# Bursts of transposes on one Trainium2 core: two chunks at once in the feed-forward stages, and a few heads later in the attention

## The chip, the core and the metric

The kernel runs on one core of a Trainium2 chip. Such a core has a matrix engine (TensorE, "PE" in the profile), three engines for elementwise work (VectorE "DVE", ScalarE "ACT", GpSimd "POOL"), and SyncE ("SP"), which here issues the DMA transfers. TensorE reads from the on-chip memory SBUF and writes to PSUM, a small memory of banks. Each engine works through its own list of instructions in order; an instruction that needs another engine's result waits for a semaphore, and everything behind it on its engine waits too. The metric is the device time in microseconds of one execution; lower is better.

## The reference

The program is a two-layer encoder trunk for 256 tokens of 1024 numbers, in float32. Each layer does

```
x = x + 1/2 * SwiGLU_1(RMSNorm(x))            # 1024 -> 2 x 2816 -> 1024
z = RMSNorm(x) @ W_in                         # 1024 -> 4352: queries, keys, values, gates
x = x + (sigmoid(gA) * (oA @ P_A) + sigmoid(gB) * (oB @ P_B)) @ W_out
x = x + 1/2 * SwiGLU_2(RMSNorm(x))
```

where SwiGLU is `(silu(x @ w_gate) * (x @ w_up)) @ w_down`. oA is a neighbourhood attention on a grid 64 tokens wide (8 heads of 64, the "grid" or "na" heads), oB a sliding-window attention of +-128 tokens (8 query heads that share 2 key and value heads, a bias by distance and a learned sink, the "sw" heads). Queries and keys are normalised per head first.

## The kernel before, in words

**Precision and matmuls.** Every float32 matrix product is done with three matmuls: each operand is split into a high part (a float32r copy by ScalarE, line 180) and a low part (the difference, by VectorE, line 181), and `three` (lines 165 to 168) adds high x high, high x low and low x high into one PSUM bank. Most are 128x128 weights against 512 columns. The 256 tokens are two tiles of 128 ("t" 0 and 1).

**Weights.** They stream from HBM through four buffers `raw`; `parts` splits each piece (two blocks of 128 rows by 512 columns) into `wh` and `wl`, six buffers each. A piece is used for tile 0, then for tile 1, and is free after that.

**The feed-forward stages** (`ffn`, four of them). The 2816 hidden columns are taken in 11 chunks of 256. For a chunk, `project` makes gate and up for both tiles (24 matmuls a tile); ScalarE takes silu (`sg`), VectorE multiplies (`hh`). `turn` then transposes the product of a chunk: four 128x128 transposes on TensorE into a PSUM bank `tp` (of two), from where the result is split into `hi` and `lo`. For chunks that PLAN marks F or G, four sums of blocks (`a`, four small VectorE additions) come first, because the products with w_down are done there with seven block products in place of eight (`sevens`); S chunks go without. The combined weights that this needs (`u` and `v`, from two DMA'd rows of w_down) are prepared ahead for three chunks: PREP says in which chunk of gate and up. The second half, `down`, uses all of it.

**The attention** (`mix`). The columns of W_in are done unit by unit in the order of ORDER: Q and K are queries, keys and values of the sliding window, q, k, v those of the grid, g the gates; the digit is the tile or the unit. An entry like a4 starts the next head: its score products (`front`) are due so many steps later. A head goes through five stations: `front` (four matmuls into the bank `sc`, then VectorE's reduction `mx`, ScalarE's exponentials, VectorE's reciprocal of the sum `sm` and GpSimd's product with `S`), `turn` (four transposes into the single bank `pt`, split into `ph` and `pl`) and `back` (four matmuls with the values into `po`).

**What sets the order.** On TensorE the order is that of the program. `defer(lag, key, fn)` puts a piece of work on a list; `tick` advances a count by one for every three 512-wide matmuls (a step, in what follows) and runs what has come due. So the lags QK_LAG (queries and keys), P_LAG (a head's transposes), V_LAG (its products with the values), H_LAG and LAST_LAG (a chunk's transposes) say how many steps of other matmuls stand between a result and its use on TensorE. On the other engines a scheduler orders the instructions when the program is built, by its own estimate of times.

Of the kernel before, what the change touches and what calls it, by code (L numbers as in the profile page):

```python
# [11 lines left out]
F32 = mybir.dt.float32  # L12
# [9 lines left out]
P = 128  # L22
# [4 lines left out]
T = S // P  # L27
KD = D // P
FC = 256
NFC = FF // FC  # L30
# [12 lines left out]
LAG = 3  # L43
H_LAG, NORM_LAG, QK_LAG, P_LAG, V_LAG, M_LAG = 7.9, 4.0, 16, 10, 7.5, 5.5
LAST_LAG = 6.1
ORDER = ("Q0 Q1 K0 K1 q1 q0 a4 k0 a5 k1 a3 v0 a1 a5 v1 a3 g0 a1 a5 g1 a4 g2 a0 g3 a0 a4 g4 a1 a5 g5 a4 "
         "g6 a0 g7")
FMAX = 3.0e38
IN_W = 4352
HEAD = 128  # L50
PLAN = "SFGFGGFGGSS"
PREP = {2: 1, 5: 3, 8: 6}
NS = sum(kind != "S" for kind in PLAN)


# [1 line left out]
def hybrid_encoder(ctx, tc, x, w_gu1, w_d1, w_in, b_gate, qk_gain, rpb, sink, t5,  # L57
                   w_bna, w_bsw, w_out, w_gu2, w_d2, c_mask, c_band, out):
    nc = tc.nc
# [7 lines left out]
    ps_tp = ctx.enter_context(tc.tile_pool(name="ps_tp", bufs=2, space=PSUM))  # L67
# [18 lines left out]
    ident = const.tile([P, P], F32, name="ident")  # L86
# [64 lines left out]
    def defer(lag, key, fn):  # L151
        later.append((now[0] + lag, len(later), key, fn))
        later.sort(key=lambda e: e[0])
# [21 lines left out]
    def flipped(ap):  # L175
        step, n = ap.ap[-1]
        return bass.AP(tensor=ap.tensor, offset=ap.offset + step * (n - 1), ap=[*ap.ap[:-1], [-step, n]])

    def split_to(hi, lo, src):
        linked("act", lambda: nc.scalar.activation(hi, src, AF.Copy))  # L180
        linked("dve", lambda: nc.vector.tensor_tensor(lo, src, hi.bitcast(F32), ALU.subtract))  # L181
# [121 lines left out]
    def ffn(l, n, w_gu, w_d, after):  # L303
        with tc.tile_pool(name="ffn", bufs=1) as fp:
            hs = {}
            SLOT = ((1, 2), (0, 3))

            def turn(c, hh):
                tp = ps_tp.tile([P, 4, P], F32, name="tp", tag="tp")
                for t in range(T):  # L310
                    for i in range(2):
                        nc.tensor.transpose(tp[:, SLOT[t][i], :], hh[:, t, i * P:(i + 1) * P], ident)  # L312
                m = 4 if PLAN[c] == "S" else 7
                hi = fp.tile([P, m, P], F32R, name=f"hi{m}", tag=f"hi{m}", bufs=NS if m == 7 else NFC - NS)
                lo = fp.tile([P, m, P], F32R, name=f"lo{m}", tag=f"lo{m}", bufs=NS if m == 7 else NFC - NS)
                if m == 7:
                    a = fp.tile([P, 8, P], F32, name="a", tag="sums", bufs=2)
                    nc.scalar.activation(a[:, :4, :], tp, AF.Copy)
                    for to, x, y, op in ((4, 0, 3, ALU.add), (6, 1, 0, ALU.subtract), (5, 4, 1, ALU.subtract),
                                         (7, 2, 5, ALU.subtract)):  # L320
                        nc.vector.tensor_tensor(a[:, to, :], a[:, x, :], a[:, y, :], op)
                    split_to(hi, lo, a[:, 1:, :])
                else:
                    with tc.high_priority(150 if c == NFC - 1 else 0):
                        split_to(hi, lo, tp)
                hs[c] = (hi, lo)
# [74 lines left out]
            def combine(acc):  # L401
# [22 lines left out]

                return rest

            for c in range(NFC):
                first = n == 0 and c == 0
                if first:
                    both, second = opening(w_gu, l)  # L430
                elif n == 0 and c == 1:
                    pieces = second
                else:
                    pieces = columns(w_gu, l, c * 512, 512)
                if c in PREP:
                    prepare(PREP[c])
                pair = act.tile([P, T, FC], F32, name="hh", tag="xg", bufs=2)
                for t in range(T):
                    ps = both[t] if first else project(t, pieces, 512)
                    sg = fp.tile([P, FC], F32, name="sg", tag="sg", bufs=2)  # L440
                    nc.scalar.activation(sg, ps[:, :FC], AF.Silu, scale=rstd[t])  # L441
                    nc.vector.scalar_tensor_tensor(pair[:, t], ps[:, FC:], rstd[t], sg, op0=ALU.mult, op1=ALU.mult)  # L442
                defer(LAST_LAG if c == NFC - 1 else H_LAG, ("h", c), lambda c=c, pair=pair: turn(c, pair))

            down()

# [15 lines left out]
    def mix(l, n, after):  # L462
        with tc.tile_pool(name="mix", bufs=1) as mp:
# [13 lines left out]
            def queries(key, ps, t, qT):  # L477
                qn = act.tile([P, NH, DH], F32, name="qn", tag="xg", bufs=2)
                normed(ps, t, NH, qn)
                qs = mp.tile([P, NH, 2, DH], F32R, name="qs", tag="qk", bufs=2)  # L480
                split_to(qs[:, :, 0, :], qs[:, :, 1, :], qn)

                def turn():
                    for half in range(2):
                        tp = ps_tp.tile([P, 4, P], F32R, name="tp", tag="tp")
                        for j in range(4):
                            nc.tensor.transpose(tp[:, j, :], qs[:, 4 * half + j].rearrange("p two d -> p (two d)"),
                                                ident_r)
                        nc.scalar.activation(qT[:, 4 * half:4 * half + 4, t * P:(t + 1) * P], flipped(tp), AF.Copy)

                defer(QK_LAG, key, turn)

            def keys(key, ps, t, nh, g, kh, kl):
                kn = mp.tile([P, NH, 2, DH], F32, name="kn", tag="qk", bufs=2)
# [21 lines left out]
            def attend(name, ins, qT, kh, kl, kidx, bias_of, vcol, ready, oT, sink_l=None):  # L516
# [11 lines left out]
                @urgent  # L528
                def front(h):
                    need(*ins)  # L530
                    if h + 2 < NH:
                        bias.append(bias_of(h + 2))
                    b = bias.pop(0)
                    least = FMAX
                    if sink_l is not None:
                        sk, least = (v[:, sink_l * NH + h:sink_l * NH + h + 1] for v in (snk, nsnk))
                    ps = ps_acc.tile([P, T, S], F32, name="sc", tag="sc", bufs=2)
                    S_ = mp.tile([P, T, S], F32, name="S", tag="S", bufs=LAG)
                    mx = small.tile([P, T], F32, name="mx", tag="mx")
                    sm = small.tile([P, T], F32, name="sm", tag="sm")  # L540
                    for t in range(T):
                        for i, k in enumerate((kh, kl)):
                            nc.tensor.matmul(ps[:, t, :], qT[:, h, t * P:(t + 1) * P], k[:, kidx(h), :],
                                             start=i == 0, stop=i == 1)
                    for t in range(T):
                        nc.vector.tensor_tensor_reduce(S_[:, t, :], ps[:, t, :], b(t), -1.0, least,  # L546
                                                       ALU.add, ALU.min, mx[:, t:t + 1])
                    for t in range(T):
                        nc.scalar.activation(S_[:, t, :], S_[:, t, :], AF.Exp, bias=mx[:, t:t + 1], scale=-1.0,  # L549
                                             accum_out=sm[:, t:t + 1])  # L550
                    if sink_l is not None:
                        es = small.tile([P, T], F32, name="es", tag="es")
                        nc.scalar.activation(es, mx, AF.Exp, bias=sk)
                        nc.vector.tensor_tensor(sm, sm, es, ALU.add)
                    nc.vector.reciprocal(sm, sm)  # L555
                    nc.gpsimd.tensor_tensor(S_, S_, sm.unsqueeze(2).to_broadcast([P, T, S]), ALU.mult)  # L556
                    defer(P_LAG, (name, h, 0), lambda: turn(h, S_))

                @urgent
                def turn(h, S_):  # L560
                    tp = ps_acc.tile([P, T, T, P], F32, name="pt", tag="pt")
                    for t in range(T):
                        for kt in range(T):
                            nc.tensor.transpose(tp[:, kt, t, :], S_[:, t, kt * P:(kt + 1) * P], ident)  # L564
                    ph = mp.tile([P, T, T, P], F32R, name="ph", tag="ph", bufs=2)
                    pl = mp.tile([P, T, T, P], F32R, name="pl", tag="pl", bufs=2)
                    split_to(ph, pl, tp)
                    defer(V_LAG, (name, h, 1), lambda: back(h, ph, pl))
# [69 lines left out]
            def na_bias(h):  # L638
                t2 = mp.tile([P, T2W], F32, name="t2", tag="t2", bufs=2)
                for r in range(2):  # L640
# [12 lines left out]
            sw = attend("sw", ("Q0", "Q1", "K0", "K1"), sqT, *skT, lambda h: h // 4, sw_bias,  # L653
                        lambda kt, h: sv[:, kt, h // 4, h % 2 * DH:h % 2 * DH + P], lambda: True, oB, sink_l=l)
            na = attend("na", ("q0", "q1", "k0", "k1"), qT, *kT, lambda h: h, na_bias,
                        lambda kt, h: va[:, kt, h, :], lambda: "v1" in done, oA)
# [10 lines left out]
            due = 0  # L667
            for token in ORDER.split():
                if token[0] == "a":
                    it, h = next(heads)  # L670
# [149 lines left out]
```

## Time and profile before

| | |
|---|---|
| median of 3 runs (lowest, highest) | 1085.79 us (1085.53, 1086.32) |
| the profiled execution | 1085.86 us |
| its span in the profile | 1084.1 us |
| TensorE busy | 1072.5 us (99%) |
| VectorE, ScalarE, GpSimd busy | 874.5, 670.7, 116.9 us |
| transposes of hh on TensorE (line 312) | 176, 271 ns each as shown |
| transposes of the heads' S (line 564) | 128, 3.8 us of idle time ahead of them |
| HBM read | 210.59 MB, 195 GB/s over the span |

The profile gives start and duration of every instruction on every engine. On TensorE durations overlap, because matmuls are pipelined: what a matmul costs is read from the distance between starts. "L564" is line 564 of the kernel; "pt<-ident,S" says what is written and read. The number in square brackets behind a row is how long its engine stood idle before it, and what ended that. The first and the second layer show the same pattern, so a place in the first layer stands for two.

### The profile page before, as it was taken

The numbers are of one execution on the slowest core, as the hardware profiler recorded it, in microseconds if no ns is written. First come the engines' busy times: TensorE is split into PE (matmuls) and PEld (weight loads), VectorE is DVE, ScalarE is ACT, GpSimd is POOL, SyncE is SP. The second block draws the span as 40 slices with busy tenths as digits, with TensorE's granted clock in tenths as the row PEclk, the third lists the DMA queues.
The fourth block names the chain that finished last, engine by engine and source line by source line (L and its number), as shares of the span: only waits on it lengthen the run. The fifth ranks groups of instructions, "written<-read, shape, count | busy, mean of one in ns | idle before, by whom it ended". The sixth has DMA issues, their size and how long they took to land.

```text
span 1084.1 us, 14710 instructions
## 1 busy us (share of the span) xinstructions
PE 1072.5 (99%) x5125; PEld 889.6 (82%) x5125; DVE 874.5 (81%) x1337; ACT 670.7 (62%) x1014; POOL 116.9 (11%) x118
## 2 busy tenths in 40 slices
PE   9999999999999999999999999999999999999998
PEld 6888888888888888888878888888888888888887
DVE  6887798888886778779978787988888766878796
ACT  6665654788764656565556665557877645656552
POOL 1000130243420000000000000003534100000000
PEclk9999999999999999999999999999999999999999
DMA  7876665755654576665657766547566555676652
GB/s 239 270 214 212 196 205 174 230 192 144 192 181 145 188 239 196 214 208 189 212 164 225 233 204 205 187 152 238 182 189 179 176 165 171 218 246 197 213 184 78
DMA packets 98827, 212.63 MB, mean 196 GB/s; under 512 B 7568, under 2 KB 13744, under 8 KB 98752
## 3 DMA queue, kind: packets, MB, share of 16 engines
q1 hardware_dynamic: 98560, 211.60, 62.1%
q8 instruction: 40, 0.66, 0.2%
q0 software_dynamic: 192, 0.08, 0.1%
q14 instruction: 35, 0.29, 0.1%
HBM read 210.59 MB, written 1.06 MB: 195 GB/s over the span
## 4 chain that ended last, share of the span: by engine, by line
PE 87%; DVE 6%; ACT 3%; DMA 2%; issue 2%; SPq 0%; POOL 0%; DVEq 0%; ACTq 0%
PE g L168 20%; PE g L166 20%; PE g L167 20%; PE acc L166 5%; PE acc L168 5%; PE acc L167 5%; DVE wl L181 2%; PE tp L312 2%; PE tp L166 1%; PE tp L167 1%; PE tp L168 1%; ACT wh L180 1%; DMA raw<-in_w_d 1%; PE g L233 1%; PE pt L564 1%
## 5 line engine op out<-in xcount | busy, mean ns | idle before, releaser
L181 DVE TENSOR_TENSOR wl<-raw,wh 128x1024 fp32r<-128x1024 f32 x336 | 403.0, 1214 | 62.5 <-ACT wh L180 61.5
L180 ACT ACTIVATE wh<-raw 128x1024 fp32r<-128x1024 f32 x336 | 345.2, 1044 | 112.0 <-PE g L168 38.7
L166 PE MATMUL g<-wh,xh 128*128 128x512 f32 (+1 forms) x976 | 386.1, 396 | 0.0
L168 PE MATMUL g<-wh,xl 128*128 128x512 f32 (+1 forms) x976 | 378.2, 388 | 0.7 <-DVE xl L181 0.7
L167 PE MATMUL g<-wl,xh 128*128 128x512 f32 (+1 forms) x976 | 377.8, 387 | 0.5 <-DVE wl L181 0.4
L168 PEld LDWEIGHTS g<-wh,xl 128*128 128x128 f32 x976 | 183.4, 188 | 40.8 <-DVE xl L181 2.1
L167 PEld LDWEIGHTS g<-wl,xh 128*128 128x128 f32 x976 | 183.8, 188 | 33.6 <-DVE wl L181 1.4
L166 PEld LDWEIGHTS g<-wh,xh 128*128 128x128 f32 x976 | 183.6, 188 | 32.5 <-DVE hh L442 0.2
L441 ACT ACTIVATE sg<-g,rs_y 128x256 f32<-128x256 f32 x88 | 41.3, 470 | 110.8 <-PE g L168 98.4
L340 DVE TENSOR_TENSOR u<-raw 128x512 f32<-128x512 f32 x64 | 43.2, 690 | 52.2 <-DMA raw<-in_w_d 51.8
L166 PE MATMUL acc<-wh,hi 128*128 128x512 f32 x180 | 71.1, 395 | 0.0
L168 PE MATMUL acc<-wh,lo 128*128 128x512 f32 x180 | 70.2, 390 | 0.0
L167 PE MATMUL acc<-wl,hi 128*128 128x512 f32 x180 | 70.1, 390 | 0.0
L172 POOL TENSOR_TENSOR rs_y<-ms,mhalf 128x1 f32<-128x1 f32 x12 | 6.7, 557 | 554.2 <-DVE ms L218 545.8
L442 DVE SCALAR_TENSOR_TENSOR hh<-g,rs_y,sg 128x256 f32<-128x256 f32 x88 | 42.1, 478 | 29.7 <-ACT sg L441 29.6
L180 ACT ACTIVATE corner<-raw 128x512 fp32r<-128x512 f32 x32 | 20.2, 631 | 49.9 <-DMA raw<-in_w_d 29.6
L556 POOL TENSOR_TENSOR S<-S,sm 128x512 f32<-128x512 f32 x32 | 37.1, 1160 | 71.8 <-DVE sm L555 45.3
L168 PEld LDWEIGHTS acc<-wh,lo 128*128 128x128 f32 x180 | 33.8, 188 | 7.2
L166 PEld LDWEIGHTS acc<-wh,hi 128*128 128x128 f32 x180 | 33.8, 188 | 6.8
L167 PEld LDWEIGHTS acc<-wl,hi 128*128 128x128 f32 x180 | 33.8, 188 | 6.7
L549 ACT ACTIVATE S<-S,mx 128x256 f32<-128x256 f32 x64 | 31.8, 498 | 7.5 <-DVE mx L546 7.4
L181 DVE TENSOR_TENSOR lo<-a,hi 128x896 fp32r<-128x896 f32 x32 | 34.7, 1084 | 0.0
(189 smaller groups left out, 1519.2 us busy)
## 6 DMA issues: line engine op xcount, KB each, us to landing
raw<-in_w_gu SPq DMA_DIRECT2D x176, 512.0 KB, 4.4
raw<-in_w_d SPq DMA_DIRECT2D x100, 512.0 KB, 4.1
raw<-in_w_in SPq DMA_DIRECT2D x64, 512.0 KB, 4.7
raw<-in_w_out SPq DMA_DIRECT2D x16, 512.0 KB, 3.6
bb<-in_b_gate SPq DMA_DIRECT2D x16, 256.0 KB, 3.5
raw<-in_w_bsw SPq DMA_DIRECT2D x8, 512.0 KB, 4.0
raw<-in_w_bna SPq DMA_DIRECT2D x8, 512.0 KB, 3.5
raw<-in_w_d SPq DMA_DIRECT2D x12, 256.0 KB, 2.7
```

The costliest lines, as they stand in the source:

```text
L166: nc.tensor.matmul(ps, xh, wh, start=first, stop=False)
L167: nc.tensor.matmul(ps, xh, wl, start=False, stop=False)
L168: nc.tensor.matmul(ps, xl, wh, start=False, stop=last)
L180: linked("act", lambda: nc.scalar.activation(hi, src, AF.Copy))
L181: linked("dve", lambda: nc.vector.tensor_tensor(lo, src, hi.bitcast(F32), ALU.subtract))
L233: nc.tensor.matmul(ps[t], a[:, k, :], b[:, k % 2, :], start=a is xh and b is wh and k == 0, stop=b is wl and k == KD - 1)
L312: nc.tensor.transpose(tp[:, SLOT[t][i], :], hh[:, t, i * P:(i + 1) * P], ident)
L340: sub = lambda to, x, y: nc.vector.tensor_tensor(to, x, y, ALU.subtract)
L441: nc.scalar.activation(sg, ps[:, :FC], AF.Silu, scale=rstd[t])
L442: nc.vector.scalar_tensor_tensor(pair[:, t], ps[:, FC:], rstd[t], sg, op0=ALU.mult, op1=ALU.mult)
L549: nc.scalar.activation(S_[:, t, :], S_[:, t, :], AF.Exp, bias=mx[:, t:t + 1], scale=-1.0, accum_out=sm[:, t:t + 1])
L556: nc.gpsimd.tensor_tensor(S_, S_, sm.unsqueeze(2).to_broadcast([P, T, S]), ALU.mult)
```

## The change

In the feed-forward stages the chunks' products wait in a list, and `turn` takes a group: after each odd chunk the two last ones are transposed together, eight transposes one behind the other into both `tp` banks, and then arranged one after the other (the new function `arrange` holds what stood in `turn`). So the pairs are 0 and 1, 2 and 3, 4 and 5, 6 and 7; the last three chunks stay single. The prepared weights are loaded and combined in chunks 3, 5 and 7 in place of 2, 5 and 8. In the attention a table MORE adds steps to four lags: 2 for the queries of the second tile of the sliding window, 1.5 for the transposes of head 4 of the sliding window, 2 and 1.5 for those of heads 4 and 5 of the grid. The first entry a4 of ORDER becomes a5.

```diff
-ORDER = ("Q0 Q1 K0 K1 q1 q0 a4 k0 a5 k1 a3 v0 a1 a5 v1 a3 g0 a1 a5 g1 a4 g2 a0 g3 a0 a4 g4 a1 a5 g5 a4 "
+MORE = {"Q1": 2, ("sw", 4): 1.5, ("na", 4): 2, ("na", 5): 1.5}
+ORDER = ("Q0 Q1 K0 K1 q1 q0 a5 k0 a5 k1 a3 v0 a1 a5 v1 a3 g0 a1 a5 g1 a4 g2 a0 g3 a0 a4 g4 a1 a5 g5 a4 "
          "g6 a0 g7")
...
-PREP = {2: 1, 5: 3, 8: 6}
+PREP = {3: 1, 5: 3, 7: 6}
...
-            def turn(c, hh):
-                tp = ps_tp.tile([P, 4, P], F32, name="tp", tag="tp")
-                for t in range(T):
-                    for i in range(2):
-                        nc.tensor.transpose(tp[:, SLOT[t][i], :], hh[:, t, i * P:(i + 1) * P], ident)
+            def turn(group):
+                tps = [ps_tp.tile([P, 4, P], F32, name="tp", tag="tp") for _ in group]
+                for (_, hh), tp in zip(group, tps):
+                    for t in range(T):
+                        for i in range(2):
+                            nc.tensor.transpose(tp[:, SLOT[t][i], :], hh[:, t, i * P:(i + 1) * P], ident)
+                for (c, _), tp in zip(group, tps):
+                    arrange(c, tp)
+
+            def arrange(c, tp):
                 m = 4 if PLAN[c] == "S" else 7
...
+            waiting = []
             for c in range(NFC):
...
-                defer(LAST_LAG if c == NFC - 1 else H_LAG, ("h", c), lambda c=c, pair=pair: turn(c, pair))
+                waiting.append((c, pair))
+                if c % 2 or c >= NFC - 3:
+                    defer(LAST_LAG if c == NFC - 1 else H_LAG, ("h", c), lambda group=waiting: turn(group))
+                    waiting = []
...
-                defer(QK_LAG, key, turn)
+                defer(QK_LAG + MORE.get(key, 0), key, turn)
...
-                    defer(P_LAG, (name, h, 0), lambda: turn(h, S_))
+                    defer(P_LAG + MORE.get((name, h), 0), (name, h, 0), lambda: turn(h, S_))
```

How it moves instructions, at three places. The first is VectorE in the second feed-forward stage, in chunk 4, from the product `hh` of its first tile to that of its second (`u` and `v` belong to the prepared weights of chunk 3, `wl` to the weights of the next chunk). Before:

```order
L442 SCALAR_TENSOR_TENSOR hh_4134<-g_4135,rs_y_3679,sg_4175 128x256
L340 TENSOR_TENSOR u_4234<-raw_4232,raw_4230 128x512
L321 TENSOR_TENSOR a_4167<-a_4167 128x128 x4
L181 TENSOR_TENSOR wl_4221<-raw_4218,wh_4220 128x1024
L181 TENSOR_TENSOR ul3_4238<-u_4234,uh3_4237 128x1024
L181 TENSOR_TENSOR wl_4227<-raw_4224,wh_4226 128x1024
L181 TENSOR_TENSOR lo7_4166<-a_4167,hi7_4165 128x896
L181 TENSOR_TENSOR wl_4323<-raw_4320,wh_4322 128x1024
L442 SCALAR_TENSOR_TENSOR hh_4134<-g_4178,rs_y_3765,sg_4203 128x256
```

With the change:

```order
L449 SCALAR_TENSOR_TENSOR hh_4119<-g_4120,rs_y_3679,sg_4175 128x256
L327 TENSOR_TENSOR a_4157<-a_4157 128x128 x3
L327 TENSOR_TENSOR a_4167<-a_4167 128x128 x2
L327 TENSOR_TENSOR a_4157<-a_4157 128x128
L327 TENSOR_TENSOR a_4167<-a_4167 128x128 x2
L182 TENSOR_TENSOR wl_4221<-raw_4218,wh_4220 128x1024
L182 TENSOR_TENSOR lo7_4156<-a_4157,hi7_4155 128x896
L182 TENSOR_TENSOR lo7_4166<-a_4167,hi7_4165 128x896
L346 TENSOR_TENSOR u_4234<-raw_4232,raw_4230 128x512
L346 TENSOR_TENSOR u_4234<-raw_4230 128x512
L182 TENSOR_TENSOR wl_4227<-raw_4224,wh_4226 128x1024
L449 SCALAR_TENSOR_TENSOR hh_4119<-g_4178,rs_y_3765,sg_4203 128x256
```

The additions and splits of two chunks stand here now, and both `u` behind them; the weight split wl_4227, the fourth piece of the next chunk, comes behind all of these. The second place is TensorE in the attention of the first layer, at the transposes of head 4 of the sliding window. Before:

```order
L166 MATMUL g<-wh,xh_1737 128x512
L167 MATMUL g<-wl,xh_1737 128x512
L168 MATMUL g<-wh,xl_1738 128x512
L564 MATMUL pt<-ident,S 128x128 x4
L166 MATMUL g<-wh,xh_1737 128x512
L167 MATMUL g<-wl,xh_1737 128x512
L168 MATMUL g<-wh,xl_1738 128x512
L166 MATMUL g<-wh,xh_1793 128x512
L167 MATMUL g<-wl,xh_1793 128x512
L168 MATMUL g<-wh,xl_1794 128x512
L543 MATMUL sc<-skT,sqT 128x256 x4
```

With the change:

```order
L167 MATMUL g<-wh,xh_1737 128x512
L168 MATMUL g<-wl,xh_1737 128x512
L169 MATMUL g<-wh,xl_1738 128x512
L167 MATMUL g<-wh,xh_1737 128x512
L168 MATMUL g<-wl,xh_1737 128x512
L169 MATMUL g<-wh,xl_1738 128x512
L574 MATMUL pt<-ident,S 128x128 x4
L553 MATMUL sc<-skT,sqT 128x256 x4
L167 MATMUL g<-wh,xh_1737 128x512
L168 MATMUL g<-wl,xh_1737 128x512
L169 MATMUL g<-wh,xl_1738 128x512
```

Six matmuls that stood behind the transposes stand ahead of them; the score product of the head two further on follows directly. The third place is VectorE earlier in the same attention, from the split of head 0 on (sm_2298 is the sum of head 1). Before:

```order
L181 TENSOR_TENSOR pl_2321<-pt_2315,ph_2320 128x512
L554 TENSOR_TENSOR sm_2298<-sm_2298,es_2307 128x2
L181 TENSOR_TENSOR wl_2566<-raw_2563,wh_2565 128x1024
L555 RECIPROCAL sm_2298<-sm_2298 128x2
L546 ISA S_2391,mx_2392<-sc_2390,t5b_2222,nsnk_97 128x256
L546 ISA mx_2392 128x1
L546 ISA S_2391,mx_2392<-sc_2390,t5b_2222,nsnk_97 128x256
L546 ISA mx_2392 128x1
L471 TENSOR_REDUCE hv_2347<-sq_2345 128x8
```

With the change:

```order
L182 TENSOR_TENSOR pl_2324<-pt_2318,ph_2323 128x512
L564 TENSOR_TENSOR sm_2298<-sm_2298,es_2307 128x2
L182 TENSOR_TENSOR wl_2566<-raw_2563,wh_2565 128x1024
L556 ISA S_2391,mx_2392<-sc_2390,t5b_2225,nsnk_97 128x256
L556 ISA mx_2392 128x1
L556 ISA S_2391,mx_2392<-sc_2390,t5b_2225,nsnk_97 128x256
L556 ISA mx_2392 128x1
L565 RECIPROCAL sm_2298<-sm_2298 128x2
```

The reciprocal of head 1 stands behind the reductions of head 2 now. On GpSimd the order is the same in both; on SyncE only the six loads for the prepared weights stand elsewhere.

## The prediction

> **What bounds the kernel now.** I read the page's busy times first, then who waited for whom, then the TensorE timeline wherever it stands still. The span is 1084.1 us and the execution itself took 1085.86 us, so 1.8 us lie outside the span; the median of the runs shown is 1085.79, 0.07 below the profiled one.
>
> ```profile
> span 1084.1 us, 14710 instructions
> PE 1072.5 (99%) x5125; PEld 889.6 (82%) x5125; DVE 874.5 (81%) x1337; ACT 670.7 (62%) x1014; POOL 116.9 (11%) x118
> PE 87%; DVE 6%; ACT 3%; DMA 2%; issue 2%; SPq 0%; POOL 0%; DVEq 0%; ACTq 0%
> ```
>
> TensorE is the bound everywhere, so time can come only from two things: its own instructions in a cheaper order, or the few places where it stops. The grouped rows and the list of waits name the stops; a number behind a releaser is microseconds in total.
>
> ```profile
> L564 PE MATMUL pt<-ident,S 128*128 128x128 f32 x128 | 19.3, 273 | 3.8 <-DVE sm L555 2.1 <-DVE pl L181 1.7
> PE sc L543 <- DVE skT L507: 0.6, 2, 0.3
> ```
>
> Both recur once per layer. The timeline of the first layer shows them one by one (start, duration):
>
> ```profile
> 225.32 0.28 PE L543 MATMUL sc<-skT,sqT 128*128 128x256 f32 x1
> 225.88 0.62 PE L543 MATMUL sc<-skT,sqT 128*128 128x256 f32 x3 [0.29 <-DVE skT L507]
> ...
> 258.97 0.39 PE L168 MATMUL g<-wh,xl 128*128 128x512 f32 x1
> 260.20 0.63 PE L564 MATMUL pt<-ident,S 128*128 128x128 f32 x4 [0.85 <-DVE pl L181]
> ...
> 297.15 0.40 PE L168 MATMUL g<-wh,xl 128*128 128x512 f32 x1
> 297.52 0.63 PE L564 MATMUL pt<-ident,S 128*128 128x128 f32 x4
> ...
> 301.75 0.28 PE L578 MATMUL po<-pl,va 128*128 128x256 f32 x1
> 303.06 0.63 PE L564 MATMUL pt<-ident,S 128*128 128x128 f32 x4 [1.04 <-DVE sm L555]
> ```
>
> A busy stream starts a 512-wide matmul every 0.227 us (24 of them in 5.44 us, rows further down). So head 4 of the sliding window starts its transposes 260.20 - 258.97 - 0.23 = 1.00 us late; head 3 of the grid 0.14 late; head 4 of the grid, behind a 256-wide matmul that takes 0.12, 303.06 - 301.75 - 0.12 = 1.19 late. The first score product stands 0.44 us between its halves (225.88 - 225.32 - 0.12), and pays some 0.1 more to fill up again: 0.55. What each waits for is VectorE:
>
> ```profile
> 225.35 0.48 DVE L507 SCALAR_TENSOR_TENSOR skT<-tp,qkg,skT 128x256 fp32r<-128x256 f32 x1
> ...
> 259.38 0.68 DVE L181 TENSOR_TENSOR pl<-pt,ph 128x512 fp32r<-128x512 f32 x1
> ...
> 302.24 0.68 DVE L181 TENSOR_TENSOR pl<-pt,ph 128x512 fp32r<-128x512 f32 x1
> ```
>
> There is one PSUM buffer "pt", so a head's transposes cannot start before the split of the head ahead (pl) has read it: that ends at 260.06 and 302.92, and TensorE starts 0.14 later each time. The second wait is listed under the reciprocal only because that ended a moment later.
>
> **The change, part by part.** (1) Grouped transposes. The instructions are the same 176, and 4 x 4 = 16 pairs of bursts become 16 bursts of eight. The trace has bursts of both lengths among the same matmuls:
>
> ```profile
> 61.44 0.60 PE L312 MATMUL tp<-ident,hh 128*128 128x128 f32 x4
> 61.80 0.49 PE L166 MATMUL g<-wh,xh 128*128 128x512 f32 x1
> 62.12 0.39 PE L167 MATMUL g<-wl,xh 128*128 128x512 f32 x1
> ...
> 63.74 0.39 PE L168 MATMUL g<-wh,xl 128*128 128x512 f32 x1
> ...
> 66.02 0.39 PE L166 MATMUL g<-wh,xh 128*128 128x512 f32 x1
> ...
> 71.46 0.39 PE L166 MATMUL g<-wh,xh 128*128 128x512 f32 x1
> ...
> 332.26 1.03 PE L703 MATMUL tp<-ident,gate 128*128 128x128 f32 x8
> 333.05 0.48 PE L166 MATMUL g<-wh,oB 128*128 128x512 f32 x1
> ...
> 334.96 0.39 PE L168 MATMUL br<-wh,oA 128*128 128x512 f32 x1
> ```
>
> From the start of four transposes to the ninth matmul behind them: 63.74 - 61.44 = 2.30 us, of which eight steps of 0.227 are 1.81, so a burst of four costs 0.49. For eight: 334.96 - 332.26 = 2.70, less 1.81, is 0.89. A pair saves 2 x 0.486 - 0.886 = 0.086, and 16 pairs 1.4 us. Part of it is sure: up to the next matmul a burst of four takes 0.36 and the second four of eight add 0.43, while the slow first step behind (0.32 in place of 0.23) is paid once. That alone is 0.5; the rest is the recovery of some steps after it. Bounds 0.5 and 1.4; I take 1.4, since the eight of L703 are the nearest row.
>
> (2) Head 4 of the sliding window, transposes two groups of three matmuls later: 6 x 0.227 = 1.36 us of matmuls that were behind the wait go ahead of it. They would then start at 260.56 where the buffer is free at 260.20. The whole 1.00 goes, 2.0 over two layers, with 0.36 us to spare. Its attention-times-values product moves along, as the order shows, so that distance stays. Bounds 0 (the split slips as well) and 2.0.
>
> (3) Head 4 of the grid, two later, behind a further score product: from 301.87 on come three matmuls, the product's four of 0.12 and three matmuls again, 1.84 us, so 303.71 against a buffer that is free at 303.06. The 1.19 go, 2.4 over two layers. The split of this head is now queued behind the next head's two reductions on VectorE (an estimate of 0.8 us, from the 0.91 between the reciprocal at 240.03 and the second reduction's end at 240.99 further down); who waits for it is head 5's transposes, and those moved later too, by the third entry. Head 3's 0.14 stays. Bounds 0 and 2.4.
>
> (4) The first score product comes a step (three matmuls, 0.68 us) later, which covers its 0.44: 1.1 over two layers. For head 1 the order takes some back: its reciprocal now stands behind two reductions, and GpSimd's product behind that:
>
> ```profile
> 240.03 0.16 DVE L555 RECIPROCAL sm<-sm 128x2 f32<-128x2 f32 x1
> ...
> 240.91 0.08 DVE L546 DVE_READ_ACCUMULATOR2_ANT mx<- 128x1 f32 x1
> ...
> 240.34 1.04 POOL L556 TENSOR_TENSOR S<-S,sm 128x512 f32<-128x512 f32 x1 [1.96 <-ACT sq L469]
> ...
> 242.74 0.60 PE L564 MATMUL pt<-ident,S 128*128 128x128 f32 x4
> ```
>
> The product would end near 240.99 + 0.31 + 1.04 = 242.3 and TensorE, 0.55 earlier, asks at 242.19: with the hand-over a wait of up to 0.3. Net 0.5 over two layers, bounds 0.5 and 1.1. The second tile's queries, whose eight transposes and two copies to sqT come two steps (six matmuls, 1.36 us) later, I cost at nothing: TensorE has the same matmuls to do meanwhile, and the first to read them is that first score product, which stands behind several steps of other matmuls in the order. If this cover went, the wait of 0.55 would be back.
>
> (5) The block rows loaded in chunks 3, 5 and 7 in place of 2, 5 and 8, and arranging two chunks at once, add no instruction. They crowd VectorE and ScalarE after the burst; what hides it is the stock of split weights. For the tightest place, the turn of chunks 2 and 3 within chunk 4, the rows of before are:
>
> ```profile
> 415.34 0.60 PE L312 MATMUL tp<-ident,hh 128*128 128x128 f32 x4
> ...
> 417.37 1.06 ACT L180 ACTIVATE wh<-raw 128x1024 fp32r<-128x1024 f32 x1 [0.80 <-PE g L168]
> ...
> 416.48 0.69 DVE L340 TENSOR_TENSOR u<-raw 128x512 f32<-128x512 f32 x1 [3.36 <-DMA raw<-in_w_d]
> ...
> 419.11 1.02 DVE L321 TENSOR_TENSOR a<-a 128x128 f32<-128x128 f32 x4
> 420.05 1.22 DVE L181 TENSOR_TENSOR wl<-raw,wh 128x1024 fp32r<-128x1024 f32 x1
> ...
> 423.45 1.08 DVE L181 TENSOR_TENSOR lo<-a,hi 128x896 fp32r<-128x896 f32 x1
> ```
>
> In the new order one weight split, two lo, two u and another weight split follow the eight additions. ScalarE's first wh would end at 417.37 + 0.43 (the longer burst) + 1.06 = 418.9; then 1.1 + 2 x 1.0 + 2 x 0.6 + 1.2 = 5.5 brings the last split to 424.4. TensorE needs it after eight transposes (0.79), the tile's 24 matmuls and 19 of the next, 43 x 0.227 = 9.8: at 415.34 + 10.6 = 425.9. So 1.5 us to spare, and I cost it at nothing. If the u wait for their DMA, the spare shrinks by that wait. The same holds for chunks 4 and 5: 8 places in all.
>
> Sum: 1.4 + 2.0 + 2.4 + 0.5 = 6.3. 1085.86 - 6.3 = 1079.6 for the profiled execution, **1079.5 us** against the median.
>
> **The rivals.** *TensorE runs into VectorE's own pace.* For it: VectorE is busy 31.93 of 37 us and 18.06 of 20 around the two waits.
>
> ```profile
> 225.00:262.00 37.00, 35.86 (x202) 30.16 (x201) 31.93 (x74) 30.01 (x67) 17.77 (x13) 1.00 0.63 188
> 284.00:304.00 20.00, 18.96 (x105) 15.99 (x104) 18.06 (x38) 14.55 (x34) 10.40 (x8) 1.00 0.66 197
> ```
>
> If its queue does not move up when TensorE comes a microsecond earlier, the next heads wait instead. Against it: much of that queue waits for TensorE itself (buffers that a matmul frees), and the 3.8 us of idle time of the pt row are nearly used up by the three heads named (2 x (1.00 + 0.14 + 1.19) less the hand-over), so the other heads have some slack. If half of (2) to (4) comes back, 4.9 / 2 = 2.4 are left and the time is 1085.8 - 1.4 - 2.4 = 1082.0.
>
> *The waits only move* (the change does not do what it says): the split slips behind the reductions, so the transposes find the buffer taken in the new place too. Then only (1) remains: 1084.4. Against it stands that both buffers are freed by instructions ahead of the reordered ones.
>
> *VectorE's burst comes too late* (slower). Place: the second weight split after the turns of chunks 2/3 and 4/5. For it: the u waited 3.36 us for DMA in the row above. With that whole wait the split is 3.36 - 1.5 = 1.9 late, at 8 places 15, and 1085.8 - 6.3 + 15 = 1094.5. It outweighs the gain once the DMA wait exceeds 1.5 + 6.3 / 8 = 2.3 us. Against it: the u now stand behind some 5 us of other work, so their DMA has that much longer.
>
> *Longer bursts of transposes lose TensorE's clock.* If eight in a row ran at half the clock they would take twice the 0.79 us from 332.26 to 333.05, 16 x 0.79 = 12.6 more, and the time would be 1085.8 - 6.3 + 12.6 = 1092.1. Against it stands the window that holds those eight; its last three numbers are the granted clock, the DMA share and GB/s:
>
> ```profile
> 331.50:335.00 3.50, 3.50 (x22) 2.96 (x21) 2.86 (x5) 2.28 (x4) 0.00 (x0) 1.00 0.50 170
> ```
>
> The Trainium skill, page "TensorE: Matmul & The Clock Gate", section "Part 4: PE-mode transpose", speaks for it: transposes, it says, do not engage the full clock, since they do not count as a busy TensorE in the same way. By that rule the trace would have to show less than the 1.00 it shows.
>
> **How the numbers follow.** Forecast 0.62, with its own range 1078.2 to 1081; running into VectorE's pace 0.20 (1081 to 1083.6 mostly); waits only move 0.07; burst too late 0.09, of which a part stays inside no change; the clock 0.02. The range that should hold 8 in 10 is 1078.2 to 1083.8: below, all bounds at their best (1.4 + 2.0 + 2.4 + 1.1 = 6.9, 1078.9) and 0.7 for what may go beside them, such as head 3's 0.14 twice; above, the first rival. 0.2% (2.2 us) is about what a measurement of this kernel can tell from no change. Faster by more than that: 0.62 + most of 0.20 = 0.82; within: 0.11; slower: 0.07.
>
> **What would show it.** In the profile after: L574 (the old L564) with an idle sum below 1.2 in place of 3.8; the score product's 0.6 near zero; bursts of eight hh with 0.79 to the next matmul; TensorE without new idle rows for wl or hh in the gate-and-up stages. A row "PE g <- DVE wl" or "<- DVE hh" of more than 2 us in total would prove the burst; a pt row still above 2.5 would prove that the waits moved.

## The result

The changed kernel takes 1078.47 us (median; 1078.21 to 1079.11), the kernel before 1086.05 us in the same comparison (1085.53 to 1086.43): a ratio of 0.9929, 95% interval 0.9914 to 0.9944. Forecast were 1079.5 us, a gain of 6.3; measured is a gain of 7.6. The profiled execution of the change is the slowest of its four, 1079.11 us, and with its span of 1077.3 us it shows 6.8 of those 7.6. The medians of the experiments leave out two runs that lie far off, one of 2785.03 us (groups alone) and one of 1333.67 us (the change with a4).

From the page of the change: the busy times, and the shares of the chain that ended last.

```profile
PE 1069.9 (99%) x5125; PEld 890.8 (83%) x5125; DVE 876.0 (81%) x1337; ACT 671.9 (62%) x1014; POOL 116.5 (11%) x118
PE 96%; DVE 2%; DMA 1%; issue 1%; ACT 0%; ACTq 0%; DVEq 0%
```

The same work is done by the same number of instructions on each of these engines, and TensorE's share of the chain went from 87% to 96%. The list of TensorE's waits that are left (who waits for whom; total, times, longest), and the grouped row of the heads' transposes, whose idle time was 3.8 us:

```profile
PE idle L117 <- DVE blank L112: 1.6, 1, 1.6
PE g L168 <- DVE wl L182: 1.1, 2, 0.7
PE g L169 <- DVE xl L182: 0.7, 1, 0.7
PE g L167 <- DVE hh L449: 0.5, 1, 0.5
L574 PE MATMUL pt<-ident,S 128*128 128x128 f32 x128 | 19.2, 272 | 0.0
```

The pt rows and the row of the first score product are gone. One row is new, the wait for hh, and the row for wl grew from 0.4 to 1.1; together they stay below the 2 us that the prediction named as the sign of its burst rival. Where the time went is read by stages. A stage ends where the first transposes of the next norm start, and the first stage is counted from the start of the span. For the attention of the first layer those rows are, of the kernel before,

```profile
185.67 0.60 PE L197 MATMUL tp<-ident,x 128*128 128x128 f32 x4
357.17 0.49 PE L197 MATMUL tp<-ident,x 128*128 128x128 f32 x3
```

and of the change

```profile
354.41 0.49 PE L198 MATMUL tp<-ident,x 128*128 128x128 f32 x3
```

with the same start at 185.67; so 171.5 and 168.7 us. The table gives all six stages (ff are the feed-forward stages; the last one ends with TensorE's last matmul), for the runs below too:

| us | ff 1 | attention 1 | ff 2 | ff 3 | attention 2 | ff 4 |
|---|---|---|---|---|---|---|
| before | 185.7 | 171.5 | 181.9 | 182.5 | 171.5 | 187.4 |
| the change | 185.7 | 168.7 | 181.4 | 182.1 | 168.7 | 187.0 |
| the change, second profile | 185.0 | 168.8 | 181.4 | 182.1 | 168.8 | 187.0 |
| groups alone | 184.8 | 171.5 | 181.7 | 182.1 | 171.4 | 187.0 |
| heads alone | 184.9 | 168.8 | 182.5 | 182.5 | 168.7 | 187.9 |
| heads and block rows in 3, 5, 7 | 185.8 | 168.7 | 183.6 | 182.5 | 168.7 | 188.2 |
| the change, block rows in 2, 5, 8 | 184.6 | 168.7 | 181.5 | 182.1 | 168.9 | 187.1 |
| the change, fewer steps | 185.2 | 171.0 | 181.4 | 182.1 | 171.0 | 187.0 |
| the change with a4 | 185.0 | 170.1 | 181.5 | 182.2 | 169.8 | 187.3 |
| three steps further | 184.2 | 169.0 | 181.3 | 182.0 | 168.7 | 186.9 |

Each attention stage gained 2.8 us, each of the last three feed-forward stages 0.4, the first nothing in this profile. The rows of the change (start, duration) that answer to those shown of before:

```profile
61.81 1.03 PE L314 MATMUL tp<-ident,hh 128*128 128x128 f32 x8
62.60 0.48 PE L167 MATMUL g<-wh,xh 128*128 128x512 f32 x1
...
64.51 0.39 PE L169 MATMUL g<-wh,xl 128*128 128x512 f32 x1
...
226.03 0.64 PE L553 MATMUL sc<-skT,sqT 128*128 128x256 f32 x4
...
259.80 0.39 PE L169 MATMUL g<-wh,xl 128*128 128x512 f32 x1
260.03 0.60 PE L574 MATMUL pt<-ident,S 128*128 128x128 f32 x4
...
301.97 0.39 PE L169 MATMUL g<-wh,xl 128*128 128x512 f32 x1
302.20 0.60 PE L574 MATMUL pt<-ident,S 128*128 128x128 f32 x4
```

The first score product runs in one piece. Head 4 of the sliding window and head 4 of the grid start their transposes one matmul step, 0.23 us, behind the matmul ahead. Eight transposes take 0.79 us to the next matmul and 2.70 to the ninth.

VectorE's splits that free the bank pt for heads 4 of the sliding window and of the grid:

```profile
258.85 0.68 DVE L182 TENSOR_TENSOR pl<-pt,ph 128x512 fp32r<-128x512 f32 x1
...
300.68 0.68 DVE L182 TENSOR_TENSOR pl<-pt,ph 128x512 fp32r<-128x512 f32 x1
```

They end at 259.53 and 301.36, where they ended at 260.06 and 302.92 before. So VectorE's queue came earlier by 0.53 at the first, as much as the first score product had lost, and by 1.56 at the second, that and the 1.00 of head 4 in front of it: it did not hold TensorE back.

The new wait is in the first feed-forward stage. TensorE and VectorE around it:

```profile
49.91 0.39 PE L169 MATMUL g<-wh,xl 128*128 128x512 f32 x1
50.78 0.50 PE L167 MATMUL g<-wh,xh 128*128 128x512 f32 x1 [0.48 <-DVE hh L449]
```

```profile
42.09 1.29 DVE L346 TENSOR_TENSOR u<-raw 128x512 f32<-128x512 f32 x2 [2.53 <-DMA raw<-in_w_d]
...
49.12 1.21 DVE L182 TENSOR_TENSOR wl<-raw,wh 128x1024 fp32r<-128x1024 f32 x1
50.26 0.47 DVE L449 SCALAR_TENSOR_TENSOR hh<-g,rs_y,sg 128x256 f32<-128x256 f32 x1
```

VectorE stood 2.53 us before u, until its block row had landed, and worked without a gap from then on; the hh that empties the bank g came 0.64 us late for TensorE (50.78 - 49.91 - 0.23).

### The profile page after: what moved, and what is told of

It reads as the page before. It is cut to its first block, busy times and chain, and to the rows that moved or that the text cites. A ratio compares the mean times of both kernels' runs of the same rounds, so it can differ in the third digit from the quotient of the medians.

```text
span 1077.3 us, 14747 instructions
## 1 busy us (share of the span) xinstructions
PE 1069.9 (99%) x5125; PEld 890.8 (83%) x5125; DVE 876.0 (81%) x1337; ACT 671.9 (62%) x1014; POOL 116.5 (11%) x118
## 4 chain that ended last, share of the span: by engine, by line
PE 96%; DVE 2%; DMA 1%; issue 1%; ACT 0%; ACTq 0%; DVEq 0%
PE g L167 21%; PE g L169 21%; PE g L168 21%; PE acc L167 5%; PE acc L169 5%; PE acc L168 5%; PE tp L314 2%; PE sc L553 1%; PE po L588 1%; PE tp L169 1%; PE tp L167 1%; PE tp L168 1%; PE pt L574 1%; DMA raw<-in_w_gu 1%; PE tp L198 1%; PE g L234 1%
## 5 line engine op out<-in xcount | busy, mean ns | idle before, releaser
L167 PEld LDWEIGHTS g<-wh,xh 128*128 128x128 f32 x976 | 183.6, 188 | 33.8 <-DVE hh L449 1.1
```

The lines of the kernel that those rows point to most:

```text
L167: nc.tensor.matmul(ps, xh, wh, start=first, stop=False)
```

## The experiments

All were run beside the kernel before (the diffs are against the change), whose median was 1085.95 us beside groups alone, heads alone, the change with block rows in chunks 2, 5 and 8, and fewer steps, and 1086.14 us beside the other four. The interval of each ratio is some 1 to 1.6 us to either side, so parts of a microsecond are read from the stages and waits of the profiles.

### Groups alone

```diff
-MORE = {"Q1": 2, ("sw", 4): 1.5, ("na", 4): 2, ("na", 5): 1.5}
+MORE = {}
-ORDER = ("Q0 Q1 K0 K1 q1 q0 a5 k0 ...
+ORDER = ("Q0 Q1 K0 K1 q1 q0 a4 k0 ...
```

> Only the feed-forward part of the change: two chunks transposed together and the block rows loaded in chunks 3, 5 and 7; the attention as before (no added steps, first entry a4). My theory: a pair saves 0.09 us, so the second, third and fourth feed-forward stage are each 0.37 to 0.44 us shorter and the two attention stages keep their 171.5 us; the first feed-forward stage gains its 0.4 and loses it in a wait of 0.6 us at the product hh of chunk 2. Total 1.2 to 1.5 below the kernel before: 1084.7. Rival (eight in a row save nothing, the trace after owes it to the attention): 1086.0, all stages as before. Rival (the attention gains because VectorE is ahead after the groups): the attention stages would be under 170.5 here too.

1084.03 us (1083.87 to 1085.12), ratio 0.9981 (0.9971 to 0.9991): 1.9 below before. Feed-forward stages 2 to 4 fell by 0.2 to 0.4 and the attention stages stayed; the heads' waits are those of before, to the tenth (who waits for whom, in this run):

```profile
PE pt L574 <- DVE sm L565: 2.1, 2, 1.0
...
PE sc L553 <- DVE skT L517: 0.6, 2, 0.3
```

The gain of the groups is there without the heads, and the attention's gain does not come from the groups. The first stage is 0.8 shorter here than in the profile of before, more than the pairs give; how that stage varies is taken up below.

### Heads alone

With `if True` every chunk is a group of its own.

```diff
-                if c % 2 or c >= NFC - 3:
+                if True:
-PREP = {3: 1, 5: 3, 7: 6}
+PREP = {2: 1, 5: 3, 8: 6}
```

> Only the attention part of the change: the added steps and a5; chunks transposed one by one, block rows loaded in chunks 2, 5 and 8 as before. My theory: the two waits for the single bank pt and the wait between the halves of the first score product go, and VectorE's queue moves up with TensorE, so each attention stage is 2.75 us shorter: 168.75 us, total 1086.05 - 5.5 = 1080.5, and the feed-forward stages keep their times. Rival (TensorE meets VectorE's own pace): half of it comes back in later heads, 1083. Rival (both parts need each other): attention above 170 us.

1080.65 us (1079.77 to 1081.93), ratio 0.9949 (0.9934 to 0.9964). The attention stages have the whole gain, 168.8 and 168.7. What was not expected: the second and the fourth feed-forward stage are 0.6 and 0.5 longer than before. TensorE there, at the transposes of chunk 1:

```profile
389.06 0.38 PE L314 MATMUL tp<-ident,hh 128*128 128x128 f32 x2
389.93 0.44 PE L314 MATMUL tp<-ident,hh 128*128 128x128 f32 x2 [0.50 <-DVE hh L449]
```

The first tile's two go, the second tile's wait for their hh. VectorE has the same order there in both kernels. Its first u, which waits for a block row, and that hh, in the kernel before,

```profile
382.28 0.69 DVE L340 TENSOR_TENSOR u<-raw 128x512 f32<-128x512 f32 x1 [3.12 <-DMA raw<-in_w_d]
...
392.18 0.47 DVE L442 SCALAR_TENSOR_TENSOR hh<-g,rs_y,sg 128x256 f32<-128x256 f32 x1
```

and in this run:

```profile
379.69 0.69 DVE L346 TENSOR_TENSOR u<-raw 128x512 f32<-128x512 f32 x1 [4.03 <-DMA raw<-in_w_d]
...
389.40 0.48 DVE L449 SCALAR_TENSOR_TENSOR hh<-g,rs_y,sg 128x256 f32<-128x256 f32 x1
```

Counted from the start of the stage (357.17 and 353.67), u starts at 25.1 and 26.0, hh at 35.0 and 35.7. TensorE came to this stage 3.5 us earlier, the block row only 2.6; from the second u on VectorE works without a gap, so its hh is late as well. Before, that hh ended only 0.15 us ahead of the transposes that read it. So the two parts of the change are not quite independent; the sum of their medians, 1.9 and 5.3 against 7.4 to 7.6 for the change, is too close to show it by itself.

### Heads alone, block rows in chunks 3, 5 and 7

```diff
-                if c % 2 or c >= NFC - 3:
+                if True:
```

> The attention part alone as in the run with only heads, chunks transposed one by one, but the block rows loaded in chunks 3, 5 and 7. In the run with only heads the second and fourth feed-forward stage lost 0.6 and 0.5 us, where the third transpose of chunk 1 waited for hh. My theory: there VectorE is behind because u, v and their splits of chunk 2 stand ahead of hh; with the rows loaded in chunk 3 this wait is gone, both stages are back at 181.9 and 187.4, and the time falls by 1.0 to 1079.6 unless the first stage takes some back at hh of chunk 2. Rival (only the group turn, which asks for that hh 0.43 us later, covers it): the wait of 0.5 to 0.7 stays, 1080.6.

1084.22 us (1081.70 to 1086.20), 1.9 below the kernel before, where heads alone were 5.3 below; by the profiles 2.1 more than heads alone. The wait at chunk 1 is gone, as the theory had it, but the time did not fall: others of up to 0.9 us have come, all at the transposes that fall into chunks 3, 5 and 7. The list of waits, and TensorE at one of them (the transposes of chunk 4, within chunk 5 of the second stage, 0.7 us late):

```profile
PE tp L314 <- DVE hh L449: 2.8, 5, 0.8
```

```profile
424.99 0.44 PE L314 MATMUL tp<-ident,hh 128*128 128x128 f32 x2 [0.56 <-DVE hh L449]
```

Chunk 5 prepares a block row in heads alone too, and there its transposes wait for nothing. So a preparing chunk is not enough to make hh late. VectorE's first u of that chunk, in heads alone and here, and here the hh:

```profile
413.81 0.69 DVE L346 TENSOR_TENSOR u<-raw 128x512 f32<-128x512 f32 x1 [3.53 <-DMA raw<-in_w_d]
```

```profile
416.38 0.69 DVE L346 TENSOR_TENSOR u<-raw 128x512 f32<-128x512 f32 x1 [5.14 <-DMA raw<-in_w_d]
...
424.45 0.48 DVE L449 SCALAR_TENSOR_TENSOR hh<-g,rs_y,sg 128x256 f32<-128x256 f32 x1
```

Counted from the start of the stage (353.67 and 354.49), u starts at 60.1 in heads alone and at 61.9 here. From u on VectorE works here without a gap, and hh starts at 70.0, 0.5 later than in heads alone. TensorE asks for it 0.7 earlier, as it lost nothing at chunk 1. So the row that lands late and the wait that went make this one; why the rows land later with this table stays open. The groups are turned in the even chunks, 2, 4, 6 and 8, so in the change no turn falls into a chunk that prepares rows; part (5) of the prediction costed the loads in 3, 5 and 7 as if they were free on their own.

### The change, block rows in chunks 2, 5 and 8

```diff
-PREP = {3: 1, 5: 3, 7: 6}
+PREP = {2: 1, 5: 3, 8: 6}
```

> The whole change, but the block rows loaded in chunks 2, 5 and 8 as before. My theory: the 0.64 us that TensorE loses at the product hh of chunk 2 in the first feed-forward stage come from VectorE standing 2.5 us at a difference u whose block row was loaded late, in chunk 3; with the rows loaded in chunk 2 this wait goes, and some of it comes back as the wait of 0.44 us for lo in the products with w_down, since the loads set the pace of that stage: 185.2 to 185.7 us for it, total 1078.0 to 1078.5. Rival (the wait comes from the additions and splits of two chunks at once): the row stays at 0.5 to 0.7 us. Rival (the tables 3, 5, 7 are what keeps the group turns from crowding VectorE in every stage): each feed-forward stage 0.5 or more longer, total above 1080.

1078.77 us (1078.27 to 1079.18), the change's own time within its spread. The wait for hh in the first stage is gone, as the theory had it, and the wait for lo that was expected in its place did not come: the stage reads 184.6 us. In all five profiles with groups and the rows in chunk 3 of that stage TensorE stands 0.4 to 0.8 us for this hh; here and in the last run, with the rows in chunk 2, it does not. Nor did a wait come in chunks 2 and 8, where groups are turned. TensorE and VectorE at the place where heads alone waited, in the second stage:

```profile
388.18 1.03 PE L314 MATMUL tp<-ident,hh 128*128 128x128 f32 x8
```

```profile
388.22 0.47 DVE L449 SCALAR_TENSOR_TENSOR hh<-g,rs_y,sg 128x256 f32<-128x256 f32 x1
```

That hh ends at 388.69. Only the last two of the eight read it, and they start 0.65 us behind the first, at 388.83; turned by itself, chunk 1 would have asked for it 0.22 behind the first, at 388.40. So the 0.43 us by which a group asks later cover it here. Chunk 0's lo, 0.60 us of VectorE's time that stands ahead of this hh in heads alone, also comes behind it now. The row itself is as late as in heads alone (its first u starts 25.9 us into the stage).

So with groups either table will do: the third edit of the feed-forward part brings nothing by itself.

### Fewer steps in the attention

```diff
-MORE = {"Q1": 2, ("sw", 4): 1.5, ("na", 4): 2, ("na", 5): 1.5}
+MORE = {("sw", 4): 0.5, ("na", 4): 2}
```

> The whole change with less of the attention part: half a step for head 4 of the sliding window (its transposes one group of three matmuls later than before, not two), two steps for head 4 of the grid but none for head 5 (its transposes six matmuls and a score product, 1.84 us, earlier than in the change), none for the second tile's queries. My theory: sw head 4 asks at 260.03 - 0.68 = 259.35 for a bank that is free at 259.53 and handed over 0.14 later: a wait of 0.3; grid head 5 asks at 306.33 - 1.84 = 304.49 for a bank free at 305.21: a wait of 0.85; the first score product goes without a wait, since a5 alone covers it. Per layer 1.15, so 2.3 above the change: 1080.8. Rival (the later queries are what freed the first score product): its 0.55 is back as well, 1081.9. Rival (head 5 waits for nothing, the split of head 4 comes earlier when asked earlier): 1079.1.

1083.42 us (1082.89 to 1084.70), ratio 0.9978 (0.9968 to 0.9987); each attention stage is 2.2 to 2.3 longer, about twice the 1.15 expected. TensorE, at head 4 of the sliding window, head 5 of the grid and head 6's products with the values:

```profile
258.60 0.39 PE L169 MATMUL g<-wh,xl 128*128 128x512 f32 x1
259.15 0.63 PE L574 MATMUL pt<-ident,S 128*128 128x128 f32 x4 [0.16 <-DVE pl L182]
...
304.10 0.39 PE L169 MATMUL g<-wh,xl 128*128 128x512 f32 x1
305.16 0.41 PE L574 MATMUL pt<-ident,S 128*128 128x128 f32 x2 [0.67 <-DVE sm L565]
...
313.44 0.39 PE L588 MATMUL po<-ph,va 128*128 128x256 f32 x1 [0.75 <-DVE o L593]
```

The two waits that were worked out are there to 0.02 us: 259.15 - 258.60 - 0.23 = 0.32 (0.3 expected) and 305.16 - 304.10 - 0.23 = 0.83 (0.85 expected), and the first score product waits for nothing without the later queries. Most of the rest is a wait that no theory had on its list, 0.75 us of idle time at po. VectorE shows why:

```profile
311.40 1.66 DVE L182 TENSOR_TENSOR wl<-raw,wh 128x1024 fp32r<-128x1024 f32 x1 [0.63 <-ACT wh L181]
312.98 0.40 DVE L593 TENSOR_TENSOR o<-o,po 64x256 f32<-64x256 f32 x1
```

With head 5 moved, the read of head 5's po was put behind a split of weights, and head 6 needs that same bank. A step that moves one head's transposes also moves its products, and the single bank po is a second place where it can catch.

### a4 again, and one step for head 4 of the grid

```diff
-MORE = {"Q1": 2, ("sw", 4): 1.5, ("na", 4): 2, ("na", 5): 1.5}
+MORE = {"Q1": 2, ("sw", 4): 1.5, ("na", 4): 1, ("na", 5): 1.5}
-ORDER = ("Q0 Q1 K0 K1 q1 q0 a5 k0 ...
+ORDER = ("Q0 Q1 K0 K1 q1 q0 a4 k0 ...
```

> The whole change, but the first entry is a4 again (the first head one step earlier) while the second tile's queries keep their two steps, and head 4 of the grid gets one step in place of two. My theory: the later queries do not cover the first score product, so its 0.55 us per layer are back (the row of skT); grid head 4 asks at 302.20 - 1.16 = 301.04 (three matmuls and a score product earlier) for a bank free at 301.36 and handed over 0.14 later, a wait of 0.45. Per layer 1.0, so 2.0 above the change: 1080.5. Rival (either of the two edits alone frees the first score product): 1079.4.

1081.18 us (1080.93 to 1081.44), ratio 0.9952 (0.9937 to 0.9967). The first score product waits again, and head 4 of the grid as long as worked out, 301.53 - 300.85 - 0.23 = 0.45:

```profile
225.17 0.61 PE L553 MATMUL sc<-skT,sqT 128*128 128x256 f32 x3 [0.28 <-DVE skT L517]
...
300.85 0.39 PE L169 MATMUL g<-wh,xl 128*128 128x512 f32 x1
301.53 0.63 PE L574 MATMUL pt<-ident,S 128*128 128x128 f32 x4 [0.29 <-DVE sm L565]
```

Together with the run before: a5 alone frees the first score product, and the later queries do nothing for it. The attention stages are 1.35 and 1.1 longer than in the change, for 1.0 expected, and the median is 2.5 above that of the change run beside it.

### The change itself, once more

> The change itself, unchanged, beside the others. My theory: between 1078.2 and 1079.1 as before, and where it differs it is the first feed-forward stage, which the loads pace: 184.6 to 185.7 us in the profile, with the waits for wl at 25 us and for hh at 50 us differing, all other stages within 0.1. Rival (the 7.6 of the median against the 6.8 of the profile are in the later stages): those differ by more than 0.2.

1078.70 us (1077.91 to 1079.45), ratio 0.9930 (0.9916 to 0.9944). Its profile differs from the first one by 0.7 us in the first feed-forward stage and by less than 0.1 in the others. Over all profiles of this study that stage reads 184.2 to 185.8 us, and the waits that it shows differ in size from run to run; in the first profile of the change it had one of 0.8 us (26.21 - 25.17 - 0.23) that the second does not have:

```profile
25.17 0.39 PE L167 MATMUL g<-wh,xh 128*128 128x512 f32 x1
26.21 0.50 PE L168 MATMUL g<-wl,xh 128*128 128x512 f32 x1 [0.66 <-DVE wl L182]
```

The two profiled executions of the change lie 0.6 us apart, and this stage accounts for it. So 7.6 by the medians against 6.8 by the first pair of profiles fits this stage's own variation; executions without a profile cannot be read by stages.

### Three steps further

```diff
-MORE = {"Q1": 2, ("sw", 4): 1.5, ("na", 4): 2, ("na", 5): 1.5}
+MORE = {"Q1": 2, ("sw", 4): 1.5, ("na", 3): 0.5, ("na", 4): 2, ("na", 5): 1.5}
-                if c % 2 or c >= NFC - 3:
+                if c % 2 or c == NFC - 1:
+PREP0 = {2: 1, 5: 3, 7: 6}
...
+                prep = PREP if n else PREP0
```

> The change and three small steps further: half a step for head 3 of the grid, whose transposes still wait 0.12 us; chunks 8 and 9 transposed together as well (one pair more per stage); in the first feed-forward stage the first block rows loaded in chunk 2 as before. My theory: 0.24 from head 3, 4 x 0.094 = 0.37 from the pairs, and 0.3 to 0.7 in the first stage, about 1.1 in all: 1077.4, the attention stages at 168.6 and each later feed-forward stage 0.1 shorter. Rival (the pair of chunks 8 and 9 crowds the last chunk, whose transposes come soon after): a wait for hi or lo in the products with w_down, 1078.5 or more.

1077.36 us (1076.95 to 1077.80), ratio 0.9917 (0.9903 to 0.9930): faster than both kernels, 1.3 below the change in the same comparison, and their runs do not overlap. Stages 2 to 4 of the feed-forward part are each some 0.1 shorter, the first has no wait for hh, and head 3 of the grid follows at one step, 0.23 us behind the matmul ahead.

The attention stages did not get shorter by the 0.1 that head 3 should have brought (169.0 and 168.7); it is too little to be told apart. The three edits were not tried one by one.

## Why the prediction was right, step by step

The time lies 1.0 us below the forecast and inside the range, on the side that was given 0.82. In the two profiles the attention gained 5.6 us, where (2) to (4) had 4.9, and the feed-forward stages 1.2, where (1) had 1.4; so the sum came as close as it did in part because one term was too small and another too large. By the prediction's own terms:

**(1) Grouped transposes, 1.4.** Right: 2.70 us to the ninth matmul, as the eight of L703 had it, and 0.37 to 0.44 us in each of the last three stages, for 4 x 0.086 = 0.34; the first gained nothing in this profile. The upper bound holds; the recovery behind a burst is paid once for eight as for four. The lower bound was added up wrongly: a pair's 0.36 - 0.43 + 0.09 is 0.02, some 0.3 for all sixteen, not 0.5.

**(2) and (3) Heads 4, 2.0 and 2.4.** Right, and shown by undoing them in steps: with a step less the waits come back at 0.32 and 0.45 us, as worked out from the distance to the split. Head 5's entry is needed: without it head 5 waits 0.83. Head 3 keeps 0.12 of its 0.14.

**(4) The first score product, 0.5 net.** Mis-sized: 1.1. The wait of 0.55 went twice, and the 0.3 that was taken off for head 1 never came. The failed step set "the product would end near 240.99 + 0.31 + 1.04 = 242.3" against a TensorE that asks 0.55 earlier, but took VectorE's 240.99 from before unmoved. VectorE and GpSimd in the change:

```profile
240.29 0.08 DVE L556 DVE_READ_ACCUMULATOR2_ANT mx<- 128x1 f32 x1
240.29 0.16 DVE L565 RECIPROCAL sm<-sm 128x2 f32<-128x2 f32 x1
...
240.59 1.04 POOL L566 TENSOR_TENSOR S<-S,sm 128x512 f32<-128x512 f32 x1 [2.62 <-ACT S L559]
```

The reductions follow TensorE's score product, so they moved up by 0.62 themselves, and the product ended at 241.63 for transposes at 242.23.

**(5) VectorE's burst, 0.** Right in its sum and wrong in its place. At the eight places named, the second weight split behind chunks 2/3 and 4/5, TensorE waits for nothing. The u waited for their DMA in the first stage a chunk ahead of the first place named, and it was the hh that came late, not a weight split. There TensorE stood 0.64 us in the first profile. How much of that the stage lost is open. The kernel before stood 0.44 us for a lo further on in this stage, which the first profile of the change does not show; yet with the rows in chunk 2 neither wait is there, and the stage reads 184.6. In the kernel before:

```profile
145.42 0.39 PE L168 MATMUL acc<-vh,lo 128*128 128x512 f32 x1
146.09 0.50 PE L166 MATMUL tp<-uh,hi 128*128 128x512 f32 x1 [0.28 <-DVE lo L181]
```

And the loads in 3, 5 and 7, costed apart from the groups, cost heads alone 3.4 us by the medians, each against its own kernel before, and 2.1 by the profiles.

**The rivals.** VectorE's own pace did not bind: the splits moved up by 0.53 and 1.56, as much as TensorE had gained ahead of them. The waits did not move to new places; that they can was shown only with head 5 put back. The loads that come too late for VectorE showed in heads alone and in its run with the rows in 3, 5 and 7; in the change the only wait of that kind is the 0.64 us of the first stage. The window of the eight transposes in the change (its last numbers are the granted clock, the DMA share and GB/s):

```profile
61.50:64.00 2.50, 2.50 (x17) 2.16 (x16) 1.41 (x6) 1.52 (x3) 0.00 (x0) 1.00 0.89 327
```

The clock stayed at 1.00 through sixteen such bursts, each 0.79 us to the next matmul, as long as the bursts of eight of before. They stand between matmuls and are never more than eight. The Trainium skill (page "TensorE: Matmul & The Clock Gate", section "Part 4: PE-mode transpose") says that transposes do not engage the full clock; the 1.00 of this trace does not agree, and a longer run of transposes was not tried.

## What to carry to other kernels

When one engine is busy 99% of the time, list the places where the distance between two starts is more than its step, and give each the one or two steps of other work that it lacks; the wait that is left after a smaller step follows by subtraction. When the bound engine comes earlier, everything that follows from its results comes earlier too: take the times of the others relative to what releases them, not from the clock of the old trace. The loads need not come earlier with it: where a helper engine waits for one, everything behind it in its queue is late, so compare when the load lands with when the bound engine asks for the helper's next product.

## What was not expected of the hardware

In the run with a4 the granted clock reads 0.95 over most of the execution, and 1.00 in the change; by windows (PE, PEld, DVE, ACT, POOL busy, then granted clock, DMA share, GB/s), of that run and of the change:

```profile
500.00:700.00 200.00, 199.30 (x908) 164.97 (x907) 166.62 (x224) 118.13 (x147) 1.10 (x2) 0.95 0.63 203
```

```profile
500.00:700.00 200.00, 199.35 (x908) 164.89 (x907) 167.12 (x225) 117.69 (x148) 1.10 (x2) 1.00 0.64 203
```

Yet TensorE did the same 908 recorded matmuls in those 200 us, and the third feed-forward stage took 182.2 us against 182.1. If its steps had followed that clock, the stage would have been some 9 us longer, an estimate from 5% of 182. So a mean granted clock of 0.95 need not be a slower TensorE. One more run, of heads alone, has a mean of 0.948 and is the fastest of its four (1079.77 us); why the clock reads so was not tried.
